# Two experts at fixed places, routing reordered round the first gather, heads of the last mixer in pairs

## The chip, the core and the metric

The kernel runs on one core of a Trainium2 chip. It is one program of some 27,000 instructions on TensorE (PE; its weight loads PEld), VectorE (DVE), ScalarE (ACT), GpSimd (POOL) and SyncE (SP), whose queue issues nearly all weight loads. The metric is the time of one execution on the device, in microseconds; the figure of a kernel is the median of its runs.

## What is computed

Two transformer blocks over 256 tokens of width 1024, in fp32. The first block has a mixer of differential attention and neighbourhood attention, and then a mixture of 32 experts, of which each token uses four:

```python
def first_block(x, c, ...):
    x = x + gate1 * norm(mixer(modulate(norm(x))))
    h = modulate(norm(x))
    logits = h @ w_router + b_router        # (256, 32)
    top 4 of 32 per token, softmax over the four
    y = sum over the four: gate_e * (swiglu_clamped(h @ w1[e] + b1[e]) @ w2[e] + b2[e])
    return x + gate2 * norm(y)
...
def second_block(x, ...):
    x = x + retention_nsa_mixer(norm(x)); x = x + swiglu_ffn(norm(x))
    x = x + hgrn2_mixer(norm(x));         x = x + swiglu_ffn(norm(x))
    return norm(x)
```

The weights of one expert are 8 MB (`w1`, 1024 x 2048) and 4 MB (`w2`, 1024 x 1024); all 32 are read, whatever the routing.

## The kernel before

**Stages.** `first_mixer` to about 185 us, `route` and `places` to about 207, the loop of `experts` to about 1172, then `second_block` (an even mixer, `ffn`, the odd mixer with its eight HGRN heads from about 1530 to 1675, `ffn`).

**Experts.** An expert's weights come as twelve tiles of 128 x 2048 fp32 (1 MB): eight of `w1` and four of `w2`, loaded by `load_e` (L787 on) from SP's queue. The 32 experts are worked off in 32 places p with fixed room: 128 slots (big), 64 (full) or 32 (quarter). `places` counts the tokens of each expert, ranks the experts by count, and gives the fullest the big places (`PM`, expert to place); `ids` (L646) is the table place to expert, which SP loads into a register (L939) before it can form the address of a place's first weight. Expert 0 is an exception: it always stands at place 0, a big one, so its weights are loaded without `ids`. If an expert gets more tokens than its place has slots, `overflow` works off the rest in a further loop.

`gather` makes, for a group of places with up to 256 slots, a one-hot matrix `oh` from the tokens' positions and multiplies it with `x` on TensorE; X is evacuated with scale and shift. For a full or a quarter place, the tokens stand still and the weight moves: 4 products of 512 columns per tile, which run side by side in two or four groups of the array's columns. For a big place, X and weight are split into high and low parts (`split_e`: `ehi` on ScalarE, `elo` on VectorE) and multiplied in three passes.

The loop `for p in range(NE)` interleaves: evacuate `hid` of p (`hs`), `w1` tiles 0 to 2 of p + 1, `w2` of p, `w1` tiles 3 to 7 of p + 1, with the scatter of p and the next gather between them. PE and SP run in the order in which this code is written (a manual schedule); the other engines are ordered by the scheduler.

**Memory for tiles.** Thirteen tile buffers take turns: eight in pool `wp` (used by all weight loads of the kernel), five in `wx`, a pool opened after the first mixer's pools are closed, on the same memory. At the start, two more tiles go into `hh` and `hl`, buffers of the mixer (`spare`). A load waits on SP until its buffer's last reader is done, and all loads behind it in the queue wait with it:

```python
wl = [self.load_e("w1", None, c, w=spare[c] if c < 2 else None) for c in range(ND)]
w20 = [self.load_e("w2", None, c) for c in range(4)]
```

**HGRN heads.** For each head the odd mixer loads one tile, makes q and f by 48 large products (hi/lo passes, L91 `acc<-hh,whi` and the like), and then builds the decay-weighted score matrix in levels L = 1, 2, 4 ... 128: VectorE multiplies halves of `qk` by running totals (L1428, L1430), and after each level TensorE makes a group of small products (`small`: eight of 32 x 32). The masked scores `at` then multiply `ip`, and the result goes through a norm over the head (ScalarE, GpSimd) into `on` (L1459). The small products of one head stand between the large ones of the next.

## Time and profile before

| | us |
|---|---|
| median of three runs | 1874.76 (1873.25 to 1874.95) |
| the profiled execution | 1873.16 |
| its span | 1871.6 |
| TensorE busy | 1726.3 (92%) |
| VectorE busy | 973.7 (52%) |
| ScalarE busy | 688.1 (37%) |
| GpSimd busy | 53.1 (3%) |
| bytes moved | 564.25 MB, mean 301 GB/s |

The busy shares are averages over stages with different limits: TensorE is busy nearly everywhere, and the transfers are near their top speed in one stage only. What bounds a stage is read from the waits in it. A busy TensorE includes products that run at a lower granted clock (PEclk, in tenths of full speed).

### The profile page before, as it was taken

To read this page: it belongs to the slowest core of one execution; us is meant where nothing else is said; L and a number is where in the kernel's file an instruction comes from. 1 tells how busy PE (TensorE), PEld (TensorE's weight loads), DVE (VectorE), ACT (ScalarE), POOL (GpSimd) and SP (SyncE) were. 2 spreads that over 40 slices of the span, in tenths; PEclk is the share of its full clock that TensorE was granted. 3 is DMA by queue.
4 is the path that set the end of the run, shared out by engine and by line. 5 is a ranking of instruction groups with operands and counts; after the bars stand their busy time and mean duration, and the time that the engine had idled before them with its cause. 6 is when DMAs were issued, how large, how long until landed. Compare 5 with 4: busy or idle time off the path is not lost. (4 is left out here: it accounts for less than half of the span.)

```text
span 1871.6 us, 27432 instructions
## 1 busy us (share of the span) xinstructions
PE 1726.3 (92%) x10671; PEld 1104.4 (59%) x10671; DVE 973.7 (52%) x1756; ACT 688.1 (37%) x1210; POOL 53.1 (3%) x101
## 2 busy tenths in 40 slices
PE   6999999999999899989986877899999999999998
PEld 4776653533543453453321211778899988779997
DVE  3535663653653563473321312577665658756655
ACT  3534551421432341351100101464544555554443
POOL 0000000000000000000000000200000001100000
PEclk8999999999999999989988878899999999999999
DMA  9784889999999999999999999723455543235530
GB/s 395 276 288 173 309 326 420 400 384 421 421 421 421 421 418 421 421 412 417 422 420 422 420 421 421 281 89 135 181 202 181 209 157 134 95 144 203 193 145 23
DMA packets 79990, 564.25 MB, mean 301 GB/s; under 512 B 8960, under 2 KB 9120, under 8 KB 13296
## 3 DMA queue, kind: packets, MB, share of 16 engines
q1 hardware_dynamic: 78800, 557.58, 74.8%
q0 software_dynamic: 1056, 4.87, 0.7%
q8 instruction: 86, 1.41, 0.3%
q14 instruction: 48, 0.39, 0.1%
HBM read 561.37 MB, written 1.05 MB: 301 GB/s over the span
## 5 line engine op out<-in xcount | busy, mean ns | idle before, releaser
L87 DVE TENSOR_TENSOR wlo<-w,whi 128x1024 fp32r<-128x1024 f32 (+1 forms) x232 | 281.1, 1215 | 191.3 <-ACT whi L86 190.9
L86 ACT CAST whi<-w 128x1024 fp32r<-128x1024 f32 (+1 forms) x232 | 241.0, 1044 | 317.1 <-PE acc L91 136.3
L91 PE MATMUL acc<-w,X 128*32 128x512 f32 (+1 forms) x1728 | 325.6, 633 | 28.2 <-DMA w<-in_w_dram 27.9
L91 PE MATMUL ps_s<-w,act 128*32 128x512 f32 (+1 forms) x864 | 164.6, 681 | 28.6 <-DMA w<-in_w_dram 24.1
L91 PEld LDWEIGHTS acc<-w,X 128*32 128x32 f32 (+1 forms) x1728 | 72.4, 124 | 191.9 <-issue 128.2
L798 DVE TENSOR_TENSOR elo<-w,ehi 128x1024 fp32r<-128x1024 f32 x120 | 145.4, 1222 | 31.2 <-ACT ehi L797 31.0
L888 DVE TENSOR_TENSOR macc<-macc,ps_t 128x512 f32<-128x512 f32 x124 | 84.5, 688 | 142.0 <-PE ps_t L91 141.9
L797 ACT CAST ehi<-w 128x1024 fp32r<-128x1024 f32 x120 | 124.8, 1050 | 63.5 <-PE acc L91 42.2
L877 DVE SCALAR_TENSOR_TENSOR yl<-ps_s,gslot,yh 128x512 fp32r<-128x512 f32 x37 | 27.3, 750 | 196.6 <-ACT yh L876 196.6
L91 PEld LDWEIGHTS ps_s<-w,act 128*32 128x32 f32 (+1 forms) x864 | 41.7, 128 | 129.1 <-issue 71.0
L91 PE MATMUL acc<-hh,whi 128*128 128x256 f32 x368 | 107.0, 291 | 2.0 <-ACT whi L86 2.0
L91 PE MATMUL acc<-hh,wlo 128*128 128x256 f32 x368 | 106.8, 290 | 0.5 <-DVE wlo L87 0.5
L91 PE MATMUL acc<-hl,whi 128*128 128x256 f32 x368 | 106.9, 290 | 0.0
L91 PE MATMUL ps_s<-hh,whi 128*128 128x256 f32 x352 | 98.6, 280 | 0.0
L91 PE MATMUL ps_s<-hl,whi 128*128 128x256 f32 x352 | 98.3, 279 | 0.0
L91 PE MATMUL ps_s<-hh,wlo 128*128 128x256 f32 x352 | 98.3, 279 | 0.0
L876 ACT ACTIVATE yh<-ps_s,gslot 128x512 fp32r<-128x512 f32 x37 | 24.9, 687 | 190.5 <-PE ps_s L91 190.5
L91 PE MATMUL ps_t<-hh,whi 128*128 128x256 f32 x320 | 89.4, 279 | 0.0
L91 PE MATMUL ps_t<-hl,whi 128*128 128x256 f32 x320 | 89.3, 279 | 0.0
L91 PE MATMUL ps_t<-hh,wlo 128*128 128x256 f32 x320 | 89.3, 279 | 0.0
L91 PEld LDWEIGHTS ps_t<-yh,ot 64*128 64x128 f32 (+1 forms) x128 | 23.6, 195 | 106.0 <-issue 60.4
L91 PEld LDWEIGHTS acc<-hh,whi 128*128 128x128 f32 x368 | 70.0, 190 | 9.2 <-issue 5.2
(426 smaller groups left out, 3246.6 us busy)
## 6 DMA issues: line engine op xcount, KB each, us to landing
w<-in_w_dram SPq DMA_DIRECT2D x384, 1024.0 KB, 19.5
w<-in_ffn_dram SPq DMA_DIRECT2D x66, 1024.0 KB, 4.8
w<-in_w_ada_dram SPq DMA_DIRECT2D x24, 1024.0 KB, 10.7
w<-in_w_in_dram SPq DMA_DIRECT2D x12, 1024.0 KB, 11.4
w<-in_even_cm_dram SPq DMA_DIRECT2D x8, 1024.0 KB, 16.6
w<-in_odd_qf_dram SPq DMA_DIRECT2D x8, 1024.0 KB, 4.8
w<-in_w_out_dram SPq DMA_DIRECT2D x4, 1024.0 KB, 7.9
w<-in_even_tm_dram SPq DMA_DIRECT2D x4, 1024.0 KB, 5.6
```

The costliest lines, as they stand in the source:

```text
L86: nc.scalar.copy(hi[:, :n], w)
L87: nc.vector.tensor_tensor(lo[:, :n], w, hi[:, :n].bitcast(F32), op=OP.subtract)
L91: self.nc.tensor.matmul(out, lhsT, rhs, start=start, stop=stop, skip_group_check=True)
L797: self.nc.scalar.copy(hi, w)
L798: self.nc.vector.tensor_tensor(lo, w, hi.bitcast(F32), op=OP.subtract)
L876: nc.scalar.activation(yh[:, m], y, AF.Copy, scale=gs)
L877: nc.vector.scalar_tensor_tensor(yl[:, m], y, gs, yh[:, m].bitcast(F32), op0=OP.mult, op1=OP.subtract)
L888: nc.vector.tensor_tensor(self.macc[:, tt, m], self.macc[:, tt, m], q, op=OP.add)
```

## The change

- **Places.** A string ORDER gives the sizes of the 32 places: four big, fifteen full and thirteen quarter ones (before: five, thirteen and fourteen). `FIXED = 2`: experts 0 and 1 stand at places 0 and 1, both of 64 slots; the ranking covers the other thirty. Loads of places 0 and 1 need no `ids`.
- **Tiles.** A pool `wy` is opened ahead of the first mixer's pools and holds two tile buffers (w11, w12) and the buffer `Xh`, in which `gt1` stands during the mixer; other small buffers of the mixer share memory (`ali` in two parts, `prow`). The first loads are those of `w1` tiles 6 and 7 into `hh` and `hl`, then tiles 0 to 5. The thirteen buffers take turns from w11 on.
- **Routing.** `s2` is multiplied into the router's weights in the first mixer; the logits are made with tokens on the partitions, so the transposes of `lT` are gone. Expert 0's positions come from its own column of logits (`m0`, `p0`, `pos0`) ahead of the mask and counts of all experts (`counts`), and its gather has two halves (ScalarE and VectorE). The places and biases are spread over expert 0's first six tiles. Expert 0's weights are not split.
- **Pairs.** Two HGRN heads share the VectorE steps and the groups of small products.
- **Turns.** `in_turns` fixes the order of score products whose halves use different rows of the array.

The diff, cut to its core:

```diff
-BIGS, FULLS = (0, 4, 9, 14, 19), (2, 3, 6, 7, 11, 12, 13, 16, 17, 18, 21, 22, 23)
-SLOTS = [128 if p in BIGS else 64 if p in FULLS else 32 for p in range(NE)]
+ORDER = "FFQ FFQBQ FFFQBQ FFFQBQ FFFQBQ FFQQQQ".replace(" ", "")
+FIXED = 2
+SLOTS = [{"B": 128, "F": 64, "Q": 32}[k] for k in ORDER]
...
+    def in_turns(self, calls):
+        last = None
+        for args in calls:
+            with self.tc.issue_after(last.ins) if last else nullcontext():
+                last = self.mm(*args)
...
     def route(self):
...
-            for dc in range(ND):
-                self.mm(pl[:NE, tt, :128], self.wr[:, dc], xT[:, dc, ts], start=(dc == 0), stop=(dc == 7))
-            nc.vector.tensor_copy(lT[:, tt], pl[:NE, tt, :128])
         with self.tc.issue_after(last.ins):
-            r = self.rx = self.rstd_of_x("nrm")
-        pt = self.bank("t")
+            for tt in range(2):
+                for dc in range(ND):
+                    self.mm(pl[:, tt, :NE], xT[:, dc, tt * 128:tt * 128 + 128], self.wr[:, dc], start=(dc == 0),
+                            stop=(dc == 7))
+        r = self.rx = self.rstd_of_x("nrm")
         lg = moe.tile([128, 2, NE], F32, name="lg", tag="over")
...
+        m0 = self.small.tile([128, 2], F32, name="m0", tag="rs")
+        nc.vector.tensor_tensor(m0, lg[:, :, 0], v8[:, :, 3], op=OP.is_ge)
+        p0 = self.bank("s")
+        self.mm(p0[:, 0:1], self.before, m0[:, 0:1], start=True)
+        self.mm(p0[:, 1:2], self.ones, m0[:, 0:1], start=False)
+        self.mm(p0[:, 1:2], self.before, m0[:, 1:2], start=False, stop=True)
+        self.pos = self.small.tile([128, 2, 1], F32, name="pos0", tag="rs")
+        nc.vector.scalar_tensor_tensor(self.pos[:, :, 0], p0[:, :2], 1.0, m0, op0=OP.add, op1=OP.mult)
+        self.ngather = 0
+        self.first = self.gather([0])
+        self.first[1].pop(0)()
...
     def places(self):
...
-        nc.vector.tensor_reduce(rank, gt[:, 1:], op=OP.add, axis=AX.X)
+        nc.vector.tensor_reduce(rank, gt[:, FIXED:], op=OP.add, axis=AX.X)
...
     def gather(self, ps):
...
+        def half(q):
+            acc = self.bank("t").rearrange("p (d s) -> p d s", d=8)[:, :4]
+            for j in range(4):
+                dc = 4 * q + j
+                for tt in range(2):
+                    self.mm(acc[:, j], self.x[:, tt, dc * 128:dc * 128 + 128], oh[:, tt, :n],
+                            start=(j == 0 and tt == 0), stop=(j == 3 and tt == 1))
+            d = slice(4 * q, 4 * q + 4)
+            if q == 0:
+                for dc in range(4):
+                    self.last_act = nc.scalar.activation(X[:, dc, :n], acc[:, dc], AF.Identity,
+                                                         bias=self.sh2[:, dc:dc + 1], scale=self.s2[:, dc:dc + 1])
+            else:
+                for op, v in ((OP.mult, self.s2), (OP.add, self.sh2)):
+                    nc.vector.tensor_tensor(X[:, d, :n], acc if op == OP.mult else X[:, d, :n],
+                                            v[:, d, None].to_broadcast([128, 4, n]), op=op)
+        if n == CAP:
+            return Xs, [onehot] + [lambda q=q: half(q) for q in range(2)]
...
     def tile_e(self):
-        k = ([*range(6), *range(8, 13), 6, 7, *range(6)] + [12, *range(6, 12), *range(6)] * NE)[self.nload]
+        k = (11, 12, 8, 9, 10, *range(8))[self.nload % 13]
...
-        return self.wx.tile([128, 2048], F32, name="w", tag=f"w{k}")
+        return (self.wx if k < 11 else self.wy).tile([128, 2048], F32, name="w", tag=f"w{k}")
...
     def experts(self):
...
-        ids = {0: None}
+        ids = {p: p for p in range(FIXED)}
...
-        wl = [self.load_e("w1", None, c, w=spare[c] if c < 2 else None) for c in range(ND)]
+        wl = {c: self.load_e("w1", 0, c, w=spare[c - 6] if c > 5 else None) for c in (6, 7, *range(6))}
...
-            with self.tc.issue_after(last_oh.ins), self.tc.issue_after(self.last_sq.ins):
-                self.halves += [self.split_e(wl[0][:, m * 1024:m * 1024 + 1024]) for m in range(2)]
...
+    def hgrn_pair(self, h0, hh, hl, ip, on, hm, ATs):
...
+        for i in range(2):
+            w = self.load_w(A["odd_qf"][h0 + i], 2048)
+            pq = acc[:, i].rearrange("p (a t) -> p a t", a=2)
...
+        pcs = [self.bank("t")[:, :384].rearrange("p (a l n) -> p a l n", a=2, l=6) for _ in range(2)]
+        pls = [self.bank("s").rearrange("p (a n) -> p a n", a=4) for _ in range(2)]
+        def small(lv, Q):
+            for i in range(2):
                 for tt in range(2):
                     for b in range(4):
-                        c = slice(tt * 128 + b * 32, tt * 128 + b * 32 + 32)
-                        self.mm(pc[b * 32:b * 32 + 32, tt, lv], ks[:, c], Q[:, c], start=True, stop=True)
+                        c = slice(i * T + tt * 128 + b * 32, i * T + tt * 128 + b * 32 + 32)
+                        self.mm(pcs[i][b * 32:b * 32 + 32, tt, lv], ks[:, c], Q[:, c], start=True, stop=True)
...
     def run(self):
...
         with ExitStack() as c:
-            self.sp = c.enter_context(tc.tile_pool(name="sp1", bufs=2))
-            self.att = c.enter_context(tc.tile_pool(name="att1", bufs=1))
-            self.scratch = self.scratch_sp
-            self.first_mixer()
-        if self.stop == 1:
-            return
-        with ExitStack() as c:
+            self.wy = c.enter_context(tc.tile_pool(name="wy", bufs=1))
+            with ExitStack() as b:
+                self.sp = b.enter_context(tc.tile_pool(name="sp1", bufs=2))
+                self.att = b.enter_context(tc.tile_pool(name="att1", bufs=1))
+                self.scratch = self.scratch_sp
+                self.first_mixer()
```

**SP, the loads round the first experts.** Names: `in_w_dram` are the expert weights, of which the first twelve are place 0's, `b1w` and `prow` small tables, `ids` the load of the next expert's number into a register. Before:

```order
L64 DMA w<-in_w_out_dram 128x2048 x4
L64 DMA w<-in_w_ada_dram 128x2x1024 x4
L790 DMA w_1716<-in_w_dram 128x2048
L790 DMA w_1717<-in_w_dram 128x2048
L790 DMA w<-in_w_dram 128x2048 x10
L964 DMA b1w<-in_b_dram 32x1024 x2
L966 DMA prow_1714<-in_prow_dram 128x512
L966 DMA prow_1715<-in_prow_dram 128x512
L939 TENSOR_LOAD ids
L939 ISA x2
L790 ISA
L790 DMA w<-in_w_dram 128x2048
```

Now:

```order
L66 DMA w<-in_w_out_dram 128x2048 x4
L66 DMA w<-in_w_ada_dram 128x2x1024 x4
L834 DMA w_1706<-in_w_dram 128x2048
L834 DMA w_1707<-in_w_dram 128x2048
L834 DMA w<-in_w_dram 128x2048 x10
L1008 DMA b1w<-in_b_dram 32x1024 x2
L1010 DMA prow_1704<-in_prow_dram 128x512
L1010 DMA prow_1705<-in_prow_dram 128x512
L834 DMA w<-in_w_dram 128x2048 x8
L983 TENSOR_LOAD ids
L983 ISA x2
L834 ISA
```

Eight loads, place 1's whole `w1`, now stand ahead of the first wait for `ids`, which before came right behind the small tables.

**PE, from the last transposes of the routing to the first products of place 0.** Names: `ps_s<-w,cs` are the modulation's products, `oh,x` the gather, `acc<-ehi,Xh` and `acc<-w,X` place 0's products with its first weight. Before:

```order
L588 MATMUL ps_t<-c_73,lT 128x32
L91 MATMUL ps_s<-w,cs 32x512 x3
L588 MATMUL ps_t<-c_73,lT 128x32
L91 MATMUL ps_s<-mask,c_73 128x32 x2
L91 MATMUL ps_s<-mask,c_73 32x32
L91 MATMUL ps_s<-mask,c_73 128x32
L91 MATMUL ps_s<-mask,c_73 32x32
L91 MATMUL ps_s<-c_73,mask 32x1 x2
L91 MATMUL ps_t<-oh,x 128x128 x8
L91 MATMUL ps_s<-PM,c_73 1x32
L91 MATMUL ps_t<-oh,x 128x128 x8
L91 MATMUL acc<-ehi,Xh 128x512 x2
```

Now:

```order
L583 MATMUL ps_t<-c_73,x 128x128 x4
L583 MATMUL ps_s<-c_73,x 128x128 x4
L93 MATMUL acc<-wr,xT 128x32 x16
L93 MATMUL ps_s<-m_1690,c_73 128x1 x3
L93 MATMUL ps_s<-mask,c_73 32x32 x2
L93 MATMUL ps_s<-c_73,mask 32x1 x2
L93 MATMUL ps_t<-oh,x 128x64 x16
L93 MATMUL acc<-w,X 64x512 x8
L93 MATMUL ps_s<-mask,c_73 128x32 x3
L93 MATMUL ps_s<-PM,c_73 1x32
L93 MATMUL acc<-w,X 64x512 x8
```

The mask's products of 128 x 32, three in number, moved from ahead of the gather to behind the first two tiles of place 0; the product that `ids` comes from (`PM`, 1 x 32) moved with them, and the modulation's products (sixteen) stand ahead of all that is shown.

**PE, last mixer, from one head to the next and from one pair to the next.** Names: `acc<-` are large products of the next projection, `ip,at` a head's result, `qs,qk` and `qk` groups of small products. Before:

```order
L91 MATMUL acc<-hh,whi 128x256
L91 MATMUL acc<-hl,whi 128x256
L91 MATMUL acc<-hh,wlo 128x256
L91 MATMUL ps_t<-ip,at_11675 128x128 x3
L91 MATMUL ps_t<-qs,qk 32x32 x8
L91 MATMUL ps_t<-qk 32x32 x8
L91 MATMUL acc<-hh,whi 128x256
L91 MATMUL acc<-hl,whi 128x256
L91 MATMUL acc<-hh,wlo 128x256
L91 MATMUL acc<-hh,whi 128x256
```

Now, twelve large products behind the first pair's `ip,at`:

```order
L93 MATMUL acc<-hh,wlo 128x256
L93 MATMUL acc<-hh,whi 128x256
L93 MATMUL ps_t<-qs,qk 32x32 x8
L93 MATMUL ps_t<-qk 32x32 x8
L93 MATMUL acc<-hl,whi 128x256
L93 MATMUL acc<-hh,wlo 128x256
L93 MATMUL ps_t<-qs,qk 32x32 x8
L93 MATMUL ps_t<-qk 32x32 x8
L93 MATMUL acc<-hh,whi 128x256
```

Two heads' first groups stand close together, with two large products between them; the later levels of both heads stand in one group of sixteen.

## Rows read from the trace of the kernel before

**Rows 1.** The page's slices: GB/s moved in each of 40 equal slices.

```profile
GB/s 395 276 288 173 309 326 420 400 384 421 421 421 421 421 418 421 421 412 417 422 420 422 420 421 421 281 89 135 181 202 181 209 157 134 95 144 203 193 145 23
```

**Rows 2.** Stretches: start:end, length, each engine's busy time, PEclk, DMA share, GB/s.

```profile
142.00:156.00 14.00, 12.67 (x60) 7.68 (x58) 9.07 (x37) 8.85 (x25) 1.08 (x2) 1.00 0.79 317
156.00:168.00 12.00, 12.00 (x59) 6.86 (x58) 7.64 (x28) 8.18 (x22) 0.00 (x0) 1.00 0.01 1
168.00:187.00 19.00, 19.00 (x92) 13.61 (x91) 8.36 (x9) 5.93 (x9) 0.76 (x2) 1.00 0.47 166
187.00:240.00 53.00, 48.46 (x274) 36.45 (x273) 36.69 (x78) 32.86 (x60) 3.98 (x8) 0.94 0.79 295
240.00:268.00 28.00, 25.69 (x134) 15.10 (x127) 22.25 (x35) 12.50 (x17) 0.00 (x0) 1.00 0.94 367
268.00:402.00 134.00, 125.98 (x602) 62.33 (x602) 70.42 (x115) 47.41 (x75) 0.00 (x0) 0.99 0.96 388
402.00:1166.00 764.00, 680.58 (x3299) 274.63 (x3295) 303.60 (x528) 176.36 (x304) 0.59 (x1) 0.92 1.01 420
```

**Rows 3.** SP's issues in order of time, and one wait (total, times, longest).

```profile
142.30 3.47 SPq L790 DMA_DIRECT2D w<-in_w_dram  x3
...
168.30 21.49 SPq L790 DMA_DIRECT2D w<-in_w_dram  x9
...
SPq L939 <- DVE ids L646: 13.9, 1, 13.9
```

**Rows 4.** TensorE in order of time, end of the routing (start, length, operation).

```profile
199.04 2.12 PE L91 MATMUL ps_s<-mask,c 128*128 128x32 f32 x10 [2.14 <-DVE mask L607]
...
201.85 3.78 PE L91 MATMUL ps_t<-oh,x 128*128 128x128 f32 x16 [0.53 <-DVE oh L753]
...
207.51 0.71 PE L91 MATMUL acc<-ehi,Xh 128*128 128x512 f32 x2
```

**Rows 5.** ScalarE in order of time, evacuations of two 64-slot experts.

```profile
296.88 1.07 ACT L812 COPY hs<-acc 128x512 f32<-128x512 f32 x2 [11.21 <-PE acc L91]
...
322.43 1.07 ACT L812 COPY hs<-acc 128x512 f32<-128x512 f32 x2 [11.09 <-PE acc L91]
```

**Rows 6.** TensorE's waits from 402 to 1166 us, and its last tile.

```profile
PE acc L91 <- DMA w<-in_w_dram: 27.9, 29, 2.2
PE ps_s L91 <- DMA w<-in_w_dram: 22.9, 26, 1.4
...
1167.26 1.06 PE L91 MATMUL ps_s<-w,act 128*32 128x512 f32 x8 [1.22 <-DMA w<-in_w_dram]
```

**Rows 7.** Four microseconds with small experts (columns as in rows 2).

```profile
1140.00:1144.00 4.00, 3.44 (x16) 0.33 (x16) 0.00 (x0) 0.00 (x0) 0.00 (x0) 0.50 1.02 424
```

**Rows 8.** TensorE in order of time there.

```profile
1139.93 1.94 PE L91 MATMUL ps_s<-w,act 128*32 128x512 f32 x8 [0.45 <-DMA w<-in_w_dram]
...
1144.90 1.06 PE L91 MATMUL ps_s<-w,act 128*32 128x512 f32 x8 [0.58 <-DMA w<-in_w_dram]
```

**Rows 9.** The last mixer's heads (columns as in rows 2).

```profile
1549.00:1648.00 99.00, 95.46 (x1335) 77.02 (x1334) 76.11 (x175) 48.65 (x133) 17.89 (x39) 1.00 0.35 119
```

**Rows 10.** TensorE in order of time, one head of the last mixer.

```profile
1552.23 0.33 PE L91 MATMUL ps_t<-qk 128*32 128x32 f32 x16
...
1552.72 0.28 PE L91 MATMUL acc<-hl,whi 128*128 128x256 f32 x1
1552.83 0.28 PE L91 MATMUL acc<-hh,wlo 128*128 128x256 f32 x1
...
1560.91 0.91 PE L91 MATMUL ps_t<-ip,at 128*128 128x128 f32 x6 [0.28 <-ACT at L1446]
1561.75 0.33 PE L91 MATMUL ps_t<-qs,qk 128*32 128x32 f32 x16
...
1562.36 0.28 PE L91 MATMUL acc<-hl,whi 128*128 128x256 f32 x1
```

**Rows 11.** ScalarE in order of time, the copy of that head's result.

```profile
1564.09 0.63 ACT L1459 ACTIVATE on<-ps_t,hrr 128x128 f32<-128x128 f32 x2 [1.49 <-POOL hrr L1457]
```

More of the change, by code (lines that the diff above doesn't have):

```diff
@@ L1 @@
 import math
-from contextlib import ExitStack
+from contextlib import ExitStack, nullcontext
 import numpy as np
@@ L398, in first_mixer @@
         dk = cm(1, 1.0)
-        ali = att.tile([128, 4, 384], F32, name="ali")
-        nc.sync.dma_start(ali, A["alibi"])
+        ali = []
+        for k in range(2):
+            ali.append(att.tile([128, 2, 384], F32, name="ali", tag="natb", bufs=2))
+            nc.sync.dma_start(ali[k], A["alibi"][:, 2 * k:2 * k + 2])
         lamv = self.small.tile([64, 4], F32, name="lamv")
@@ L526, in scores @@
         sps = [self.bank("s").rearrange("p (a k) -> p a k", a=2) for _ in range(2)]
-        for qt in range(2):
-            for m in range(2):
-                r = slice(m * 64, m * 64 + 64)
-                self.mm(sps[m][:, qt], q[r, qt * 128:qt * 128 + 128], k[r], start=(qt == 0), stop=(qt == 1))
+        rs = [slice(m * 64, m * 64 + 64) for m in range(2)]
+        self.in_turns([(sps[m][:, qt], q[rs[m], qt * 128:qt * 128 + 128], k[rs[m]], qt == 0, qt == 1)
+                       for qt in range(2) for m in range(2)])
         return sps
@@ L606, in route @@
                                     f8[:, tt, 0:4, None].to_broadcast([128, 4, NE]), op=OP.is_equal)
[L607 to L614 removed]
+            self.last_mask = nc.vector.tensor_reduce(mask[:, tt], eq[:, tt].rearrange("p k e -> p e k"), op=OP.add,
+                                                     axis=AX.X)
         pc = self.bank("s")
@@ L645, in places @@
         self.ids = moe.tile([1, NE], I32, name="ids")
-        nc.vector.tensor_copy(self.ids, pi[0:1, :NE])
+        self.placed = nc.vector.tensor_copy(self.ids, pi[0:1, :NE])
+        nc.vector.scalar_tensor_tensor(pos, pp[:, :2 * NE].rearrange("p (a e) -> p a e", a=2), 1.0, mask,
+                                       op0=OP.add, op1=OP.mult)
         yield
@@ L1412, in odd_mixer @@
+        small(0, qs)
+        tot = f
+        lv = 1
+        L = 1
+        while L <= 128:
+            if L <= 16:
+                small(lv, qp)
+            for i in range(2):
+                if L == 32:
                     for tt in range(2):
                         for b in range(2):
-                            c = tt * 128 + b * 64
-                            self.mm(pl[b * 64:b * 64 + 32, tt, b * 64 + 32:b * 64 + 64], ks[:, c:c + 32],
+                            c = i * T + tt * 128 + b * 64
+                            self.mm(pls[i][b * 64:b * 64 + 32, tt, b * 64 + 32:b * 64 + 64], ks[:, c:c + 32],
@@ L1434, in odd_mixer @@
+            nc.vector.tensor_tensor(v, v, tv[:, :, :, None].to_broadcast([128, 2, nb, L]), op=OP.mult)
+            nt = att.tile([128, nb], F32, name=f"tot{L}", bufs=2)
+            nc.vector.tensor_tensor(nt, tv[:, 0], tv[:, 1], op=OP.mult)
+            tot = nt
+            L *= 2
+            lv += 1
+        for i in range(2):
+            h = h0 + i
+            hs = slice(h * 128, h * 128 + 128)
+            pc, pl = pcs[i], pls[i]
             tm = att.tile([128, 2, 6, 32], F32, name="tm", bufs=2)
@@ L1627, in prep @@
     c0[:, 672:704] = np.array(SLOTS) * cap // CAP
-    order = [p for w in (128, 64, 32) for p in range(1, NE) if SLOTS[p] == w]
-    c0[:, 704] = 99
+    order = [p for w in (128, 64, 32) for p in range(FIXED, NE) if SLOTS[p] == w]
+    c0[:, 704:704 + FIXED] = 99 + e[:FIXED]
     for r, q in enumerate(order):
```

233 lines of the change are left out of this document (108 added, 125 removed).

## The prediction, made before the changed kernel ran

> **What bounds the kernel now.** I read the page's slices first [rows 1]: from slice 10 to slice 25 (421 to 1170 us; a slice is 46.8) the transfers stand at 412 to 422 GB/s, ahead of and behind that mostly far lower. That is the expert stage: 32 experts, each with twelve tiles of 1,048,576 bytes, 384 tiles; at 421 GB/s one takes 2.49 us, all 956 us, over half of the span. The table by stretches [rows 2] says where this stream has holes. From 402 us on there are none (420 GB/s, the engines' share 1.01). Before 402 us I count for each stretch its length times (1 - GB/s / 421): 3.5, 12.0, 11.5, 15.9, 3.6 and 10.5 us, in all **57.0 us** in which the queue could have carried expert weights and did not. The SP rows [rows 3] say why: three loads at 142 us, nothing until 168.3, nine until 189.8, and then 13.9 us of waiting for `ids`, the number of the next expert.
>
> Is TensorE a second bound? From 402 to 1166 us its waits for weights add up to 27.9 + 22.9 = 51 us [rows 6], and the last tile is waited for too: so the transfers end the stage and TensorE has some 50 us to spare. Two experts of 64 slots are evacuated 25.55 us apart [rows 5], while twelve tiles need 29.9. In the second block it is the reverse: weights are there, and TensorE runs through its products one after the other.
>
> So a hole in the stream that is closed before about 250 us shortens the span one to one, as long as TensorE does not fall behind; in the second block only products, their interruptions and waits count.
>
> **The change part by part.** *(1) Loads ahead of the routing.* I go through the hole list again with the order's releases.
> - 142 to 156: one more tile is free (the mixer's buffers give two, a pool opened before the mixer two), so 5.4 tiles instead of 4.4: busy to about 155.6. Then it is empty to 169, since the next tile's memory belongs to the attention until its last product. I take 169 (168.3 was the first release before, and 172 would cost 3 more): hole 13.4.
> - 169 to 190: eight tiles instead of three, five of them free at once, the other three released as before by the splits of the output weights and the first ada product: 19.9 of 21 us, hole 1.1.
> - From 190 the small loads (0.75 MB, 1.8 us) and expert 1's first three tiles, which no longer wait for `ids`: busy to 199.3. The next tile needs the memory of expert 0's first, which TensorE must have used.
> - When does expert 0 start on TensorE? Now 207.5, 5.7 us after the start of its gather at 201.85 [rows 4]. Its gather is now of 64 slots instead of 128, its weights need no split, and the way from the logits to the gather loses two transposes, and the wait for the mask of all experts (2.14 us there). Against that, all sixteen ada products stand ahead of the transposes. I take 204.5; the ends are 202 and 207.5 (nothing gained). Its first tile is used by 204.5 + 25.55 / 12 = 206.6: hole 7.3.
> - Six tiles follow (expert 1's last five, expert 2's first), to 221.6. The wait for `ids` now stands ahead of the sixth only; the product that `ids` comes from is queued on TensorE behind two of expert 0's tiles, so about 210, before that tile's memory is free. Behind the wait on SP stands only expert 2.
> - The tile after that needs expert 1's first to have been used. Expert 0's eight tiles take at most 8/12 of 25.55 = 17.0 us, and the two further gathers and the tables in between some 5.7 (priced as the first gather's stretch): 204.5 + 17.0 + 5.7 + 2.1 = 229.3: hole 7.7.
>
> Sum 13.4 + 1.1 + 7.3 + 7.7 = 29.5, and 0.5 for the ends: 30. *(2) The order of sizes.* Two big experts now stand at 0 and 4, and the stream still loses 14 us from 240 to 402 [rows 2]; in the new order the first big one is seventh, after two small and four of 64 slots. From 229 on TensorE gains 29.9 - 25.55 = 4.3 us on the stream with each of 64; a small one's products run in four groups of columns at once instead of two, so half of 25.55 and 17 us gained at the most, of which I take 13; two gathers cost some 6 each: 3 x 4.3 + 2 x 13 - 12 = 27 us made up by then, against a lag of at most thirteen tiles (32 us) at 229. So I put the loss there at nothing; if the cover is too thin it is up to 14 again. The mix (one big and one small expert become two of 64) leaves TensorE's total about the same. The stage's gain: 57 - 30 = **27 us**. Bounds: 3 (late start), 3 (attention), 5 (tables) and 14 (order) are the four ways to lose, 6 the way to gain (a start at 202 and shorter tables): together 25; three quarters of that would leave 8, and 33 is the best.
>
> *(3) Head pairs in the last mixer.* TensorE is busy for 95.5 of 99 us there [rows 9]. A group of small products between two large ones costs more than its work: from the start of one group to the second large product behind it 0.49 us, and 0.61 where two groups stand together; a large product alone is 0.11 [rows 10]. So a group merged into another costs 0.12 and not 0.49 - 0.11 = 0.38: 0.26 saved, and about 0.05 more for the gap ahead. By the order the groups fall from 65 to 38: 27 x 0.31 = 8.4 us. Against it: a pair holds two banks of each of two kinds, so the next pair's first small product waits until both heads' results are copied out: 3.8 us from the product with `ip` (1560.91) to the end of the copy (1564.09 + 0.63) [rows 10, 11], of which three products of each head and twelve large products cover about 3.1 for the first head, and the second head's copy comes later: some 0.8 us at each of three joints. Net **-6 us**; bounds -9, and +6 if each joint waits the whole 3.8 and the chain's first and last pair lie bare.
>
> *(4) The rest.* The turns of the score products change no count, the split of the bias table adds one DMA ahead of 142 us, and the scaling of the router's weights one DVE step in a mixer in which TensorE is the busy engine: nothing, with -2 to +1. At the stage's end five loads use other tiles, so that the next block's first loads start a little earlier, behind the experts in the queue: nothing.
>
> Sum: -27 - 6 = -33 us on the profiled 1873.16, so 1840.2; this run lies 1.6 under the median of 1874.76, so **1842 us**.
>
> **A rule against it.** In stretches with small experts TensorE's granted clock falls: 0.50 from 1140 to 1144 us, the lower of the two levels, 1.2 of 2.4 GHz, and the same four products of a small expert with its second weights take 1.94 us there and 1.06 at 1144.90 [rows 7, 8]; ahead of both the engine waited for weights. Its mean from 402 us is 0.92 [rows 2]. The Trainium skill ("TensorE: Matmul & The Clock Gate", section on HAM oscillation) says that waiting for a transfer before every group of products keeps the engine cold. By that rule a kernel whose TensorE waits more would run colder; the trace agrees for the small experts, and shows the engine warm again once it has work queued. What it would do here is rival D.
>
> **The rivals.** *B: the hole comes back at the first big expert.* TensorE is not caught up at place 6, the thirteen tiles fill up and the 14 us between 240 and 402 remain. For it: this is what the trace shows for the order now; against: the 27 us made up above. Gain 27 - 14 + 6 = 19: 1856 us. *C: the pair's banks serialise the last mixer.* Part 3 becomes +6 instead of -6: 1854. For it: the static order puts only twelve large products ahead of the next pair's first small ones; against: a pair's projection, a quarter of 99 us, covers the chain otherwise, and VectorE has fewer and longer steps. *D: slower.* Place: the expert loop; mechanism: clock. TensorE's work from 207.5 to 1167, less its 51 us of waiting, is 194.5 us at 0.99 and 713 at 0.92 [rows 2, 6], about 849 us at full clock. At a mean clock c it ends at 204.5 + 849 / c; slower than before it is once that passes 1167 + 6, at c below 0.88. At 0.85 it would be 1203, 30 us over, so about 1905. Against: an engine that lags does not wait, so it is warm. *E: the change doesn't do what it says*: a fixed expert draws more than 64 tokens and the overflow loop reads weights again, at 30 us an expert at the least: over 1870. By the reference's routing of these inputs the two have 33 and 37 tokens.
>
> **How the numbers follow.** The forecast 0.56, B 0.20, C 0.16, D 0.04, E 0.01; 0.03 for smaller failures that end near zero. The forecast's own range is 1831 to 1850. For eight in ten I reach over B and C: 1829 to 1860. Faster by over 0.2% (3.7 us, about what a measurement here tells from no change): the forecast, B, C and most of the small failures, 0.94; within: 0.02; slower: D, E and the rest, 0.04.
>
> **What would show it.** Loads of expert 1 at about 190 without a wait for `ids`; expert 0's first product near 204.5 and its last tile near 227; 421 GB/s from about 230 on without the loss between 268 and 402; the last tile's product near 1140 instead of 1167. In the last mixer 93 us instead of 99, and fewer groups of small products. Wrong would be: a rate under 400 GB/s in any stretch from 260 to 1100, waits of the small products for copies of `on`, or a mean clock under 0.88 in the loop.

## The result, and the profile after

The changed kernel takes **1852.22 us** (median of four runs, 1848.9 to 1853.42) against 1874.86 for the kernel before on the same chip; the ratio is 0.9872, with a 95% interval of 0.9849 to 0.9895. The prediction said 1842 with a range of 1829 to 1860. The profiled execution took 1848.9, its span is 1847.3: 24.3 us less than the span before.

The stages by marks that both traces have (us; the mixer's end is the first product of the modulation behind it, the even mixer runs from the restart behind the experts to its `ffn`):

| | before | after | difference |
|---|---|---|---|
| first mixer ends | 185.4 | 180.9 | -4.5 |
| from there to the last `w2` product of the experts | 983.0 | 963.3 | -19.7 |
| from there to the restart of TensorE | 12.2 | 12.1 | -0.1 |
| even mixer | 146.3 | 150.4 | +4.1 |
| first `ffn` | 188.1 | 188.1 | 0.0 |
| odd mixer (HGRN heads) | 159.4 | 155.4 | -4.0 |
| the rest | 197.3 | 197.2 | -0.1 |

The page of after, its slices (GB/s in 40 equal slices, 46.2 us each); they answer to [rows 1]:

```profile
GB/s 393 292 292 280 270 401 421 420 421 421 420 421 421 420 421 421 421 421 421 421 416 420 421 421 416 208 92 114 186 203 186 216 152 134 95 156 206 194 138 23
```

The loss in slices 8 and 9 of before (400, 384) is gone: from slice 7 to slice 25 the stream runs at 416 to 421 GB/s. The same stretches as in [rows 2], of after (columns as there: PE, PEld, DVE, ACT, POOL busy, PEclk, DMA share, GB/s):

```profile
142.00:156.00 14.00, 13.86 (x68) 7.82 (x68) 9.56 (x40) 9.63 (x29) 1.08 (x2) 1.00 0.80 332
156.00:168.00 12.00, 12.00 (x58) 7.49 (x59) 6.00 (x21) 7.06 (x16) 0.00 (x0) 1.00 0.06 23
168.00:187.00 19.00, 19.00 (x110) 13.25 (x109) 10.82 (x12) 8.79 (x13) 1.52 (x4) 1.00 1.01 420
187.00:240.00 53.00, 51.55 (x276) 28.19 (x275) 18.26 (x70) 8.29 (x22) 2.26 (x6) 0.87 0.76 284
240.00:268.00 28.00, 26.20 (x138) 12.26 (x138) 8.36 (x20) 5.83 (x13) 0.00 (x0) 1.00 0.96 397
268.00:402.00 134.00, 122.48 (x609) 53.60 (x606) 61.91 (x105) 37.00 (x62) 0.00 (x0) 0.97 1.01 421
402.00:1166.00 764.00, 670.62 (x3280) 286.35 (x3279) 321.46 (x543) 195.82 (x333) 9.49 (x10) 0.94 1.01 418
```

Counted as in the prediction, length times (1 - GB/s / 421), the holes are 3.0, 11.3, 0.0, 17.2, 1.6 and 0.0: 33.1 us where 30 was forecast and 57.0 stood before. The last `w2` product ends at 1144.16 instead of 1168.32, 24.2 earlier, and the holes have shrunk by 23.9: as a book-keeping the list is right. What makes them shrink is another question, and the runs below answer half of it otherwise than the prediction did.

SP in order of time (start, length of the group): the first three loads of expert 1 follow the small tables at once, with no wait for `ids`, where [rows 3] had 13.9 us of it. The next two groups each wait for a buffer that TensorE must have used: they start at 204.21, where the forecast had 206.6, and at 226.74, where it had 229.3.

```profile
183.58 2.58 SPq L1008 DMA_DIRECT2D b1w<-in_b_dram  x2
186.25 0.85 SPq L1010 DMA_DIRECT2D prow<-in_prow_dram  x2
187.19 1.33 SPq L834 DMA_DIRECT2D w<-in_w_dram  x3
...
204.21 13.11 SPq L834 DMA_DIRECT2D w<-in_w_dram  x6
...
226.74 4.95 SPq L834 DMA_DIRECT2D w<-in_w_dram  x3
```

TensorE in order of time, end of the routing, against [rows 4]; the last row is ScalarE's: it starts to copy expert 0's sums (`hs`) when TensorE has used the last tile of its `w1`.

```profile
193.46 7.09 PE L93 MATMUL ps_t<-oh,x 128*128 128x64 f32 x32
200.49 5.64 PE L93 MATMUL acc<-w,X 128*64 128x512 f32 x16
...
206.99 3.65 PE L93 MATMUL acc<-w,X 128*64 128x512 f32 x16
...
217.43 1.90 PE L93 MATMUL ps_t<-oh,x 128*128 128x64 f32 x16
219.25 1.94 PE L93 MATMUL acc<-w,X 128*64 128x512 f32 x8
...
225.03 1.07 ACT L856 COPY hs<-acc 128x512 f32<-128x512 f32 x2 [4.32 <-PE acc L93]
```

Expert 0 starts at 200.49, 4 us ahead of the forecast 204.5, but its gather of 32 products takes 7.09 us; 16 of the same kind take 1.90 at 217.43, so 32 would take 3.8. The stretches there (columns as above) show why:

```profile
190.00:193.00 3.00, 1.63 (x11) 1.57 (x11) 2.39 (x18) 0.68 (x4) 0.00 (x0) 0.65 1.04 373
193.00:204.00 11.00, 10.92 (x50) 8.25 (x50) 3.27 (x15) 1.29 (x4) 1.36 (x4) 0.50 0.52 215
204.00:207.00 3.00, 3.00 (x20) 1.32 (x16) 0.05 (x1) 0.00 (x0) 0.00 (x0) 0.91 0.53 205
```

TensorE was busy for 1.63 of the 3 us from 190, while VectorE chose the top four, and the granted clock fell there to 0.50, the lower of its two levels (1.2 of 2.4 GHz), until about 204. The first two tiles of `w1` took 5.64 us there, where the next two took 3.65. So half of the earlier start was lost again, and `w1` was used up at 225.0, where the forecast had 227. In before the gather stood at the lower level too:

```profile
199.00:205.00 6.00, 5.44 (x29) 5.16 (x29) 3.98 (x13) 1.01 (x3) 0.00 (x0) 0.50 1.01 360
```

and TensorE, behind that stretch:

```profile
205.70 2.05 PE L91 MATMUL ps_t<-oh,x 128*128 128x128 f32 x16
```

Sixteen of its products of 128 columns took 3.78 us at that level [rows 4], and the next sixteen took 2.05 at full clock. Sixteen of 64 columns take 1.90 at full clock now, so halving the columns, which the prediction counted as a gain, saves next to nothing.

### The profile page after: what moved, and what is told of

Its sections match the earlier page's. It is cut to its first block, busy times and chain, and to the rows that moved or that the text cites. A ratio compares the mean times of both kernels' runs of the same rounds, so it can differ in the third digit from the quotient of the medians.

```text
span 1847.3 us, 27208 instructions
## 1 busy us (share of the span) xinstructions
PE 1699.0 (92%) x10655; PEld 1085.6 (59%) x10655; DVE 934.0 (51%) x1666; ACT 658.6 (36%) x1172; POOL 53.6 (3%) x101
## 5 line engine op out<-in xcount | busy, mean ns | idle before, releaser
L93 PE MATMUL acc<-w,X 128*64 128x512 f32 (+1 forms) x1792 | 344.9, 621 | 25.5 <-DMA w<-in_w_dram 24.7
L93 PE MATMUL ps_s<-w,act 128*64 128x512 f32 (+1 forms) x896 | 168.8, 637 | 30.4 <-DMA w<-in_w_dram 24.9
L93 PEld LDWEIGHTS acc<-w,X 128*64 128x64 f32 (+1 forms) x1792 | 78.7, 125 | 199.2 <-issue 133.1
L842 DVE TENSOR_TENSOR elo<-w,ehi 128x1024 fp32r<-128x1024 f32 x96 | 116.3, 1221 | 18.0 <-ACT ehi L841 16.7
L93 PEld LDWEIGHTS ps_s<-w,act 128*64 128x64 f32 (+1 forms) x896 | 45.1, 127 | 133.5 <-issue 79.8
L841 ACT CAST ehi<-w 128x1024 fp32r<-128x1024 f32 x96 | 99.9, 1050 | 50.9 <-PE acc L93 34.7
L920 ACT ACTIVATE yh<-ps_s,gslot 128x512 fp32r<-128x512 f32 x36 | 24.3, 687 | 194.1 <-PE ps_s L93 187.5
```

What stands on the lines that cost most here:

```text
L93: self.last_mm = self.nc.tensor.matmul(out, lhsT, rhs, start=start, stop=stop, skip_group_check=True)
L841: self.nc.scalar.copy(hi, w)
L842: self.nc.vector.tensor_tensor(lo, w, hi.bitcast(F32), op=OP.subtract)
L920: nc.scalar.activation(yh[:, m], y, AF.Copy, scale=gs)
```

## The experiments

Two theories of the experts' 20 us stood against each other. The prediction's: each hole that is closed ahead of 250 us counts by itself, so the early loads bring about half and the new sizes the other half. The rival (S): with thirteen buffers in turn, a load waits for TensorE to use the tile thirteen back; a hole closed early comes back later, and what counts is how soon TensorE catches up with the stream, which the sizes set.

**The sizes alone**, in the kernel before:

```diff
-BIGS, FULLS = (0, 4, 9, 14, 19), (2, 3, 6, 7, 11, 12, 13, 16, 17, 18, 21, 22, 23)
+ORDER = "FFQ FFQBQ FFFQBQ FFFQBQ FFFQBQ FFQQQQ".replace(" ", "")
...
-                self.halves += [self.split_e(wl[0][:, m * 1024:m * 1024 + 1024]) for m in range(2)]
```

> The kernel before with the new sizes of the places alone (ORDER; expert 0 stays at place 0, now with 64 slots and so without split weights; expert 1 is ranked and its loads wait for ids; routing, mixers, tiles and heads as before). Theory S (sizes): what places the weight stream is the moment at which TensorE has used the first tile of the second expert, since every buffer is full until then; that moment comes some 8 us earlier with a small first expert, and the losses between 240 and 402 us go because no big expert stands at place 4. Then most of the gain is here: 18 to 21 us faster than before, 1854 to 1857, and the wait for ids at 209 us does no harm. Theory L (loads, the prediction's first point): the stream gains hole by hole from the loads ahead of the routing, and the order is worth only the 14 us between 240 and 402: about 1861, with the hole of 13.9 us ahead of 209 fully lost.

1857.61 us, ratio 0.9908 (0.9891 to 0.9925). The mixer's end to the last `w2` product takes 967.9 instead of 983.0: -15.0, three quarters of the 19.7, with the loads and `ids` as before. Its stretches (columns as above):

```profile
168.00:187.00 19.00, 19.00 (x88) 13.25 (x86) 9.01 (x9) 6.80 (x9) 0.76 (x2) 1.00 0.46 170
187.00:240.00 53.00, 49.97 (x273) 27.85 (x274) 19.51 (x69) 15.16 (x40) 2.98 (x8) 0.87 0.88 333
240.00:268.00 28.00, 26.88 (x142) 11.90 (x138) 7.81 (x18) 6.35 (x14) 0.00 (x0) 1.00 0.99 411
268.00:402.00 134.00, 125.01 (x602) 54.40 (x603) 55.47 (x92) 33.80 (x57) 0.00 (x0) 0.96 1.01 421
```

From 240 on the holes come to 0.7 us instead of the 14.1 of before, though at 168 to 187 the stream runs at 170 GB/s, much as before (166). The prediction's list had put 14 on the order, S 18 to 21 on the sizes: the 15.0 lie near the list, and this run alone does not decide between the two. The next ones take the early loads away.

**The wait for `ids` put back** ahead of expert 1, in the changed kernel:

```diff
-        ids = {p: p for p in range(FIXED)}
+        ids = {0: 0}
```

> The changed kernel, but the second expert's number is taken from the table, so that its loads wait for ids again. Theory L: three tiles (7.5 us) are no longer loaded ahead of the routing, the hole ahead of 206 us grows by them, 7 us or more slower than the changed kernel: about 1859. Theory S: the hole grows ahead of 208 us, but the one from 222 to 227 us shrinks by the same amount, because the tile behind it waits for TensorE's use of the second expert's first tile either way: 0 to 2 us slower, 1852 to 1854, with the next issue at about 227 us as before.

1854.85 us, 0.9893 (0.9876 to 0.9910); mixer's end to last `w2` 965.6, 2.3 more than the changed kernel. The wait itself is long (first row: total, times, longest), and SP's loads behind it (start, length) begin 22.7 us later than in the changed kernel:

```profile
SPq L983 <- DVE ids L665: 20.3, 1, 20.3
...
209.85 8.84 SPq L834 DMA_DIRECT2D w<-in_w_dram  x9
...
228.14 3.22 SPq L834 DMA_DIRECT2D w<-in_w_dram  x2
```

and the stretches behind it (columns as above):

```profile
187.00:240.00 53.00, 51.54 (x280) 28.99 (x280) 18.74 (x70) 8.72 (x22) 2.25 (x6) 0.87 0.64 256
240.00:268.00 28.00, 26.20 (x140) 12.08 (x138) 8.85 (x20) 6.52 (x14) 0.00 (x0) 1.00 1.01 420
```

Not all of the 20.3 us are lost time: the changed kernel's queue, too, issues nothing from 188.5 to 204.21, with its buffers full. What the wait holds back is three tiles, 7.5 us of the stream. It then issues nine loads in one go, the next load, which waits for TensorE, comes at 228.14 instead of 226.74, and the next stretch runs at 420 instead of 397. So 7.5 us cost 2.3 here, a little more than S had said (0 to 2) and far less than theory L (7 or more). How sharp the 2.3 is stays open: it comes from one trace each, and two traces of one program can differ by 1.8 in this stage (see the pairs alone).

**The first big expert at place 2** instead of 6 (counted from 0):

```diff
-ORDER = "FFQ FFQBQ FFFQBQ FFFQBQ FFFQBQ FFQQQQ".replace(" ", "")
+ORDER = "FFB FFQQQ FFFQBQ FFFQBQ FFFQBQ FFQQQQ".replace(" ", "")
```

> The changed kernel with places 2 and 6 exchanged (the first big expert is third instead of seventh, a small one stands in its old place; all counts of sizes the same). Theory S: TensorE has not made up its lag when the first big expert comes, the buffers fill up and the stream loses 12 to 18 us between 260 and 400 us, as in the kernel before: 1864 to 1870. If the order of the sizes is of no weight and only the early loads count (theory L at its purest): within 2 us of the changed kernel, 1852.

1860.86 us, 0.9925 (0.9909 to 0.9942). Mixer's end to last `w2` takes 974.6, 11.3 more than the changed kernel with the same mix of sizes and the same early loads (S had said 12 to 18), and 9 us of it stand where the prediction's rival B had put them. That the whole lies under S's 1864 fits with a wait of 3 us behind the experts, treated below, which this kernel does not have.

```profile
240.00:268.00 28.00, 26.71 (x119) 15.51 (x116) 16.06 (x31) 14.53 (x23) 0.00 (x0) 1.00 0.90 367
268.00:402.00 134.00, 128.07 (x645) 57.10 (x643) 65.55 (x108) 37.05 (x60) 0.00 (x0) 0.99 0.98 393
```

**The two early buffers taken away** (`wy` stays, but w11 and w12 lie in `wx` as the other three):

```diff
-        return (self.wx if k < 11 else self.wy).tile([128, 2048], F32, name="w", tag=f"w{k}")
+        return self.wx.tile([128, 2048], F32, name="w", tag=f"w{k}")
```

> The changed kernel with its two early buffers back in the pool that opens after the mixer: two tiles instead of four can be loaded at 140 us, still thirteen buffers from 170 on. Theory S: the two tiles are loaded later and the hole ahead of 206 us shrinks by as much, since the stream's place at 227 us is set by TensorE and the number of buffers: 0 to 2 us slower, about 1853. Theory L: 5 us slower, 1857.

1851.85 us, 0.9882 (0.9864 to 0.9899): no difference that can be told. At 142 to 156 the rate falls from 332 to 204 GB/s, at 187 to 240 it rises from 284 to 331, and the last `w2` product ends at 1144.4 as before.

**One buffer less**, twelve in turn:

```diff
-        k = (11, 12, 8, 9, 10, *range(8))[self.nload % 13]
+        k = (11, 12, 8, 9, *range(8))[self.nload % 12]
```

> The changed kernel with twelve instead of thirteen buffers that take turns. Theory S: the stream stands one tile further back when TensorE uses the second expert's first tile, once and for all: 2.5 us slower, 1855; no new losses after 260 us if the order leaves cover at the big experts. If the cover at the big experts is thin, as rival B of the prediction had it, each of the four big experts adds a loss and it is 8 us slower or more. If the number of buffers is of no weight: within 1 us.

1854.18 us, 0.9896 (0.9878 to 0.9914); mixer's end to last `w2` 965.1, 1.8 more, where one tile takes 2.49; from 268 to 402 us the stream runs at 421 GB/s as in the changed kernel. So the cover at the big experts is not thin; that a buffer counts one tile, once, fits, but 1.8 us is no more than the scatter of the stage.

**The pairs alone**, in the kernel before (`hgrn_pair` in place of the loop over heads):

```diff
-        for h in range(8):
...
+        for h0 in range(0, 8, 2):
+            self.hgrn_pair(h0, hh, hl, ip, on, hm, ATs)
```

> The kernel before with the head pairs of the last mixer alone. Theory P: the pairs bring what the two traces show, 4.0 us between the last mixer's first transpose and the next one's (159.4 to 155.4), and the 4 us that the even mixer loses in the changed kernel have nothing to do with them: 1871 us, even mixer 146.3 as before. Rival: the gain is an accident of the order of the whole program, or the even mixer's loss comes with the pairs: within 1 us of before, or the even mixer at 150.

1872.51 us, 0.9993 (0.9983 to 1.0002), ten runs. In its trace the odd mixer takes 155.5 instead of 159.4, the 4.0 of the changed kernel; the whole gains 0.7. So the trace shows theory P's 4.0, and the times show what the rival had said, within 1 us. The stages ahead of it, in which the program is the same, took 2.6 us more in this execution (expert stage +1.8, even mixer +0.8), which is their scatter. Why ten runs show no more than 0.7 stays open.

**The turns alone taken out**: in `in_turns` the products are issued without `issue_after`.

```diff
-            with self.tc.issue_after(last.ins) if last else nullcontext():
-                last = self.mm(*args)
+            self.mm(*args)
```

> The changed kernel without the fixed turns of the score products (the products stand as the scheduler puts them, as in the kernel before). Theory T: the first mixer's 3.3 to 4.4 us (end at 180.9 to 182.0 instead of 185.4) come from the turns: it ends at 184 to 185 again, and the whole is 2 to 4 us slower, 1855. The even mixer, where the prediction saw -2 to +1, changes by less than 1. Rival: the mixer's gain comes from the other edits in it (memory of small buffers): it ends at 182 as before, and the time stays.

1852.95 us, 0.9890 (0.9872 to 0.9908), not to be told from the changed kernel as a whole; but the mixer ends at 184.3 in its trace, at 184.4 to 185.6 in the three others without turns, and at 180.8 to 182.5 in all ten traces with them. In the stretch from 142 to 156 us TensorE is busy for 12.76 us without them and for 13.86 with them. So the turns are worth 2 to 3 us in the mixer; that they reach the end of the program is not shown.

**Filler products** in the routing, to keep TensorE's clock up for the gather:

```diff
+        warm = self.acc()
+        with self.tc.issue_after(self.last_mm.ins):
+            for k in range(3):
+                self.mm(warm[:, k % 2], self.ident, self.x[:, k % 2, 0:512], start=True, stop=True)
```

> The changed kernel with three further products of 128 x 512 behind the logits' (of x with the identity, into a free accumulator that nobody reads; they add work and leave nothing out), in the time in which TensorE otherwise waits for the four best of each token. Theory W: the first gather and the first two tiles of the first expert run at the lower clock (0.50 from 193 to 204 us; 7.1 us for the gather and 5.6 for the two tiles, where the same instructions take 3.9 and 3.7 at full clock), because the routing ahead of them is small products and waiting; if the clock stays up, the first expert is through 4 to 5 us earlier, the stream's next issue comes at 222 instead of 226.7, and all of it reaches the end: 1847 to 1849. Rival: the clock falls all the same (0.50 in the gather as before), and the products only delay the chain: 0 to 1 us slower. If the stream were placed by the loads ahead of the routing and not by TensorE, a faster first expert would bring 1 to 2 us at most.

1850.75 us (1846.54 to 1855.91), 0.9871 (0.9852 to 0.9890): no difference that can be told. TensorE in order of time:

```profile
191.59 5.47 PE L93 MATMUL acc<-x,c 128*128 128x512 f32 x6
...
198.65 5.57 PE L93 MATMUL ps_t<-oh,x 128*128 128x64 f32 x32 [0.60 <-DVE oh L780]
204.15 5.13 PE L93 MATMUL acc<-w,X 128*64 128x512 f32 x16
```

The fillers, 5.47 us long, ran at the lower level themselves (granted clock 0.51 from 191.6 to 197), stood ahead of expert 0's mask and put the gather 5.2 us back; it then took 5.57 instead of 7.09.

**The transposes not held back** behind the ada products, so that these fill the wait:

```diff
-                with self.tc.issue_after(self.last_mm.ins):
+                with nullcontext():
```

> The changed kernel, but the transposes of the routing are no longer held behind all sixteen modulation products; seven of these then stand between transposes and logits, as in the kernel before. Theory W: larger products among the small ones keep TensorE's clock up, the first gather takes 4 to 5 us instead of 7.1, and the first expert is through 2 to 3 us earlier: about 1849. Rival: the clock falls as before (0.50 in the gather), and the products only stand in the way of the logits: 0 to 2 us slower, 1851 to 1853.

1853.16 us, 0.9882 (0.9865 to 0.9898). The clock stays at 1.00 to 193, but the gather falls to the lower level all the same (7.09 us) and starts 2.7 us later. Neither way brought the gather's 3.3 us back.

**Where the even mixer's 4 us are.** TensorE in order of time in the changed kernel, at the restart behind the experts; the last column is the wait ahead of the row and what ended it ("issue": nothing that the profile shows):

```profile
1157.46 0.48 PE L162 MATMUL ps_t<-c,x 128*128 128x128 f32 x1
1160.90 0.69 PE L162 MATMUL ps_t<-c,x 128*128 128x128 f32 x2 [2.96 <-issue]
```

In the kernel before these transposes run through without a wait. The place lies some instructions behind the jump over the overflow loop. Theory I: TensorE's instructions come late there, depending on where the place falls in the program. Sixteen products more ahead of it, whose results are overwritten, move all that stands behind them:

```diff
+            if dc == 0 and p in (28, 29):
+                for k in range(8):
+                    self.mm(hids[p][0][0:32, 0], Xs[p][:, 0], w[:, 0:512], start=True)
```

> The changed kernel with the first product of places 28 and 29 made nine times instead of once (each starts the accumulation anew, so the last one counts; sixteen small products more, in places where TensorE waits for weights). They do nothing but move all later TensorE instructions further back in the program. Theory I (instructions): the 3.0 us that TensorE waits for nothing visible at the start of the second block (idle before the sixth transpose) is the arrival of its next instructions behind the jump over the overflow loop; it hangs on where the jump's target lies. Then it goes: 3.7 us instead of 6.9 from the first transpose to the first product, 3 us faster than the changed kernel, about 1848. Rival: the wait is for the tokens or weights (it comes with the earlier end of the experts): it stays, 1851 to 1852.

1849.92 us, 0.9857 (0.9840 to 0.9873): 2.3 less by the medians, with intervals that overlap. In the trace the wait is gone:

```profile
1158.16 0.42 PE L162 MATMUL ps_s<-c,x 128*128 128x128 f32 x1
1158.49 0.90 PE L162 MATMUL ps_t<-c,x 128*128 128x128 f32 x3
1159.19 0.85 PE L162 MATMUL ps_s<-c,x 128*128 128x128 f32 x3
```

From the restart to the first product it is 3.71 us instead of 6.93, as in before (3.71). In all three kernels with the sixteen products it is 3.4 to 3.7; in the others made from the changed kernel it is 5.3 to 6.9, but for `big_early` (3.7) and `warm` (3.3, where the restart itself came some 4 us later). That the wait goes when the code moves is shown; that it is the arrival of instructions is argued from it.

**Both**, `shift` and the free transposes:

> The two edits together, as the candidate for a version that beats the changed kernel. If both theories hold: 1846. If only theory I holds: 1848 to 1849. If neither: 1851 to 1853.

1849.01 us, 0.9864 (0.9847 to 0.9880): as `shift`.

**The joints of the pairs.** The waits of TensorE among the heads of the changed kernel, 1525 to 1640 us (total, times, longest):

```profile
PE ps_t L93 <- ACT on L1534: 3.0, 3, 1.1
PE ps_t L1425 <- ACT on L1534: 1.6, 2, 0.9
PE ps_t L93 <- ACT qk L1459: 1.6, 2, 0.8
PE ps_t L93 <- DVE qs L1460: 1.3, 1, 1.3
```

The first line is the wait for copies of `on` that the prediction had named from [rows 10, 11], three joints of 1.0. And it has a consequence that was not foreseen. In `shift`, whose odd mixer took 159.5, TensorE in order of time behind the first joint:

```profile
1553.03 0.33 PE L93 MATMUL ps_t<-qs,qk 128*32 128x32 f32 x16 [1.00 <-ACT on L1537]
...
1554.71 0.44 PE L93 MATMUL ps_t<-qs,qk 128*32 128x32 f32 x16 [0.79 <-ACT qk L1462]
...
1555.68 0.42 PE L93 MATMUL acc<-hl,whi 128*128 128x256 f32 x1
1555.89 0.41 PE L93 MATMUL acc<-hh,wlo 128*128 128x256 f32 x1
```

and the stretch from there (columns as above), first of `shift`:

```profile
1555.30:1561.10 5.80, 5.80 (x90) 5.22 (x84) 2.78 (x4) 1.18 (x2) 0.00 (x0) 0.50 0.01 3
```

A large product takes 0.41 there instead of 0.28, and the granted clock is 0.50, the lower level, for 5.8 us; in `both`, whose program is the same there, the profile shows 1.00 behind the same waits. Among the eleven traces with pairs ahead of the last run, four have no such stretch (odd mixer 155.4 to 155.5), six have one behind a joint (156.7 to 156.9), and this one has two (159.5): 1.4 to 4.1 us, in seven traces of eleven. The two kernels with single heads have none. The Trainium skill ("TensorE: Matmul & The Clock Gate", section on a second HAM failure mode) describes, for bf16 products of 512 columns, a clock that goes up and down where TensorE idles briefly between groups of products while its PSUM banks go round. These traces agree in part: the products are fp32, and the clock falls once or twice behind such a wait (1.00 and 0.79 us), in seven traces of eleven. The last run takes the wait away by its bank, on top of `both`:

```diff
-            po = self.bank("t").rearrange("p (a e) -> p a e", a=4)
+            po = self.bank("s").rearrange("p (a e) -> p a e", a=4)
```

> The kernel `both` with one change in the last mixer: a head's result (`ip,at`) goes into a bank of kind s instead of kind t, so that the next pair's first small groups no longer need the copies of `on`; the order then puts these groups ahead of `ip,at`. In `both` the odd mixer took 155.4 us, with three waits of 1.0 us for `on` at the joints, and in seven of the eleven traces with pairs the large products right behind a joint ran at the lower clock for 3 to 5 us (0.41 instead of 0.28 us each), which cost 1.4 to 4.1 us more (156.7 to 159.5). Theory J, the joints' waits are what is missing of the 6 us: the waits for `on` are gone, no large product of the pairs takes 0.41, the odd mixer takes 151.5 to 153.5, the whole about 1843 to 1846. Rival K, the chain of ScalarE (sigmoids, `qk`) sets the joint: the wait moves to `qk` or `qs` with the same length, the odd mixer stays at 155 to 157, the whole at 1848 to 1850. Rival L, the third use of the s banks makes the later levels wait for the copies instead: over 157, the whole over 1850.

**1846.52 us** (1846.32 to 1848.03), 0.9851 (0.9836 to 0.9867): all five runs lie under the fastest of the changed kernel (1848.9); from `both` (1847.7 to 1850.82) it is 2.5 by the medians, with ranges and intervals that overlap a little. The same waits of TensorE, 1525 to 1640 us:

```profile
PE ps_t L93 <- DVE qk L1502: 2.0, 2, 1.5
PE ps_t L1428 <- DVE on L1424: 1.9, 2, 1.2
PE ps_t L93 <- DVE qs L1463: 1.9, 1, 1.9
```

The waits for `on` at the joints are gone, and the odd mixer takes 154.1 in its trace: less than the 155.4 of the undisturbed traces, though not the 151.5 to 153.5 of theory J, since VectorE's `qk` and `qs` now come last at the joints (K in part). No large product among the heads runs at the lower clock in this trace; that the bank prevents it is not shown, since four traces of eleven had no fall with the wait in place.

## Why the prediction was right, and where it was off

The sign and the places were right; of the size two thirds came, 22.6 us by the medians where 33 was forecast. The median lies in the stated range of 1829 to 1860, but 2.2 us above the forecast's own 1831 to 1850: it is covered by the room that was left for the rivals B and C, and neither of them happened as a whole. That, and two misses in (4) that cancel, is luck. By its steps:

- **(1) and (2), the expert stage: 27 forecast, 19.7 measured** from the mixer's end. The holes came as listed: 14.3 for 13.4 up to 168 us, 0.0 for 1.1, 18.8 for 15.5 behind that. Expert 0 started 4 us ahead of the forecast and was through its `w1` 2 us ahead of it, because its first two tiles ran at the lower clock (5.64 us for 3.65). Wrong was the premise that **a hole closed before 250 us shortens the span one to one**. It holds for the sum of all holes, and not for one: three tiles (7.5 us) held back by the wait for `ids` cost 2.3, two buffers filled ahead of 156 us nothing that can be told. The list itself had the reason: its last hole, from 221.6 to 229.3, ends when TensorE has used a tile, whatever was loaded before. The sizes made 15.0 of the 19.7, for the 14 that the list gave the order. So the early loads and the new routing, to which it gave the other half (27 less 14), are the mis-sized term: 2.3 by putting the wait back, 4.7 at most by what the sizes leave. The two were not taken apart. The stage's end came 24.2 earlier where 27 was forecast, and 4.5 of that stem from a mixer that ends earlier, which the sum did not have.
- **Rival B** did not happen, for the reason given: TensorE had caught up at place 6 (421 GB/s from 268 on). With the big expert at place 2 it did.
- **(3) the pairs: -6 forecast, -4.0 in the trace, less in seven traces of eleven.** The direction of both terms was right. The wait at a joint was put at 0.8 and is 1.0 for `on`, with up to 0.8 more for `qk` behind it: 4.6 us in all where 2.4 stood in the sum. Waits of the small products for copies of `on`, which the prediction had named as a sign of being wrong, are thus there, at a size near the forecast one. Not in the sum was that the clock falls behind a joint in seven of eleven traces. Rival C, the banks as a loss of 6, is refuted as a whole, but its mechanism was there: with the bank exchanged, the odd mixer gains 5.3 against before.
- **(4) the rest: nothing forecast.** The turns bring 2 to 3 us in the mixer, and the wait at the restart takes 3.0 of the even mixer's 4.1; the last 1 us was not traced. The turns had been dismissed because they change no count of products in a mixer where TensorE is busy anyway; but the stretch 142 to 156 had 12.67 us of busy time in 14 [rows 2], and has 13.86 now.
- **Rival D** (the clock in the loop) did not come: its mean is 0.94 against 0.92 in [rows 2]. **E** did not come either: 384 expert tiles were loaded, none twice.

Sum of the profiled executions: -4.5 - 19.7 + 4.1 - 4.0 - 0.2 = -24.3. The profiled execution of the changed kernel is the fastest of its four, 3.3 us under the median. Clock falls at the joints as in the other traces would give such a difference, but the other three runs have no trace, so this stays open, as does why `pairs_only` gains only 0.7 as a whole.

## What to carry to other kernels

Where loads go round a ring of buffers, a hole ahead of the point at which the reader catches up is not a cost by itself: ask which load waits for which use, one ring back, and put small work first so that the reader catches up sooner. Merging small groups of products saves their joints, but if the merged group must wait for a bank, the wait can be paid a second time in clock, as in seven traces of eleven here; give the result that is copied out last a bank that the next round does not need first. Before 3 us are put down to a change, look whether TensorE waits for nothing visible behind a jump, and move the code once.

## What the runs showed of the hardware that was not expected

- Behind the jump at the end of the expert loop TensorE waited 2.96 us for nothing that the profile shows, in some programs and not in others; with sixteen products more ahead of it, it was gone.
- In the routing the granted clock was 0.50 from 193 to 204 us: 32 products of the gather took 7.09 us, where 16 take 1.90 at 217 us. Three filler products of 512 columns, put in to prevent that, ran at the lower level themselves and took 5.47 us.
- A gather of half the columns was hardly faster at full clock: sixteen products of 128 columns took 2.05 us in before, sixteen of 64 columns take 1.90.
- Behind the same joint of the same code the granted clock was 1.00 in some traces and 0.50 in others, for 5.8 us in the trace shown, though the waits ahead of it (1.00 and 0.79 us) were the same.
